# Starting the linear branch's states beside attention, and three pauses in attention's first steps

## The chip, the cores and the metric

The kernel runs on one core of a Trainium2 chip. The metric is the device time of one execution in microseconds (us). Five engines work side by side, each through its own queue in order: TensorE (PE, with its weight loads as PEld), VectorE (DVE), ScalarE (ACT), GpSimd (POOL) and SyncE (SP), which issues most of the DMAs.

## What is computed

One inference step of a two-layer backbone on 128 context tokens and 256 latent tokens, 384 columns in all, in float32. Each layer normalises its input, projects it once, runs three token mixers, merges them by sigmoid gates, and ends in a feed-forward part. The mixers are a windowed attention with a sink, a bidirectional gated linear attention (GLA), and a pooling mixer:

```python
o_a = _latent_attention(_rope_2d(qa), _rope_2d(ka), va, kc, vc, sink)
o_b, _, _ = _gla_bidir(qb, kb, vb, la_f, la_b, st[:, 0], st[:, 1])
o_b = _rmsnorm(o_b, p['g_gla_out']).reshape(B, T, GLA_VW) * jax.nn.silu(rb)
o_c = _pool_mix(uc, p['w_pool'], p['pool_scale'])
mixed = (jax.nn.sigmoid(ga) * (o_a @ p['w_br_a']) + jax.nn.sigmoid(gb) * (o_b @ p['w_br_b'])
         + jax.nn.sigmoid(gc) * (o_c @ p['w_br_c']))
# in the GLA, per chunk:
inter = jnp.einsum('bhtd,bhde->bhte', q_ * jnp.exp(b_), S)
S_new = jnp.exp(b_[:, :, -1, :])[..., None] * S + jnp.einsum('bhsd,bhse->bhde', k_ * jnp.exp(b_last - b_), v_)
```

The final GLA states of the context tokens are an output too.

## The kernel before

**Segments.** The order of the whole program is written out by hand, as a list of segments. A segment takes one unit of weights (128x1024 values) and does its matmuls (`mm3`, line 219: 24 matmuls of 384 columns). Each float32 weight is split into a high part `wh` (ACT, line 151) and a low part `wl` (DVE, line 155); `pump` puts out the split on ACT ahead of a segment, and `run_low` the subtraction on DVE, as a rule in the middle of the next segment.

**Threads and ticks.** Everything that isn't a weight product lives in generators. `tick` first puts out what stands in `self.late` (`flush`), then advances every thread to its next `yield`, in the order in which the threads were started. A segment ticks twice: in the middle (after 12 of 24 matmuls in `mm3`; after 16 of 24 in the products of a branch, `b_fn`, line 1429) and at its end. After the middle tick comes `run_low`. In `b_fn` the two evacuations `finish` on DVE (line 1443) come after the last matmul and so ahead of the end tick. What a thread puts into `self.late` at a middle tick is put out at the start of the end tick, and what it puts there at an end tick at the start of the next middle tick.

In this text ticks are counted from the end of the segment that starts attention (tick 1). Four segments of the GLA's values follow (ticks 2 to 9), four of `rb` (10 to 17), and branch c (18 to 41), six ticks for each of its four parts: two gates (`g0`, `g1`) and a product `b_fn`. So middle ticks are even; the middle ticks of `b_fn` in branch c are 22, 28, 34 and 40, its end ticks 23, 29, 35 and 41. Branch a has its first two gates at ticks 42 to 45; its first product begins with `before_a`, which joins attention, and has ticks 46 and 47.

**Attention** (`attn`) goes through 24 heads-by-blocks in steps s = 0 to 29, one to a tick, from tick 13 on. An even step scores two heads (two matmuls into two banks that are held until the exponentials are put out; mask, row maximum and its scaling on DVE, lines 1078 to 1082) and multiplies the probabilities of an earlier pair with the values (`pv`, line 1120). An odd step puts out the exponentials of the pair (line 1091). Every step from 4 on transposes one head's probabilities (`trans`, line 1109), which ACT copies out (line 1110), and every step from 2 on scales one head's (lines 1097 to 1099). The output of `pv` is split by `split_out`: the high part by ACT at once (line 251), the low part by DVE through `self.late` (line 252). Both read the same PSUM bank.

**The GLA** (`gla`) started 20 ticks earlier and comes ahead of attention in each tick. Its products of ticks 18, 24 and 29 (96 small matmuls, line 762) fill two banks each, which DVE reads by `copy_predicated` (line 838). At tick 30 the copies of line 859 are due, and then it waits for attention. Behind that wait lie the states: their decays (lines 867 to 880), eight transposes (line 891) into two banks, copied out by ACT (line 893), the state products (line 906) into two banks, read by ACT (line 909) and DVE (line 915), and the decays of the queries (lines 923 and following). After them it waits again, at line 933, for attention and for `c_done`, which `before_a` sets, and then makes the branch's output.

**PSUM.** All these small products share four banks (`psa`), handed out in turn, without those that are held. Whoever gets a bank waits until all readers of its former content are done. The threads get their banks in the order of emission, so a thread that takes more or fewer steps shifts who follows whom.

Of the kernel before, what the change touches and what calls it, by code (L numbers as in the profile page):

```python
# [30 lines left out]
class Kern:  # L31
# [715 lines left out]
    def gla(self, l, st):  # L747
# [109 lines left out]
                yield  # L857
        for j in range(4):
            nc.vector.tensor_copy(A[32 * j:32 * j + 32, :, 32 * j:32 * j + 32], Dg[32 * j:32 * j + 32])
        while not st.get("attn_done"):  # L860
            yield

        S0 = [self.t(f"S0{d}", [128, 2, 128]) for d in range(2)]
        for d in range(2):
# [138 lines left out]
    def attn(self, l, st):  # L1003
# [62 lines left out]
        def score(u):  # L1066
            blk, j, v = units[u]
            W = 128 if blk == 0 else 384
            kk = st["k"][:, 0:128] if blk == 0 else st["KA"]
            hs = slice(64 * v, 64 * v + 64)  # L1070
            h = v * 4 + j
            ps = self.psa(hold=True)
            bank = (self.sa_i - 1) % 4
            nc.tensor.matmul(ps[:, 0:W], q[hs, j, blk * 128:blk * 128 + 128], kk[hs, :])  # L1074
            if blk:
                mt = 2 - blk
                msl = ps[:, mt * 128:mt * 128 + 128]
                nc.vector.tensor_tensor(msl, msl, self.amask[:, blk - 1, :], op=ALU.add)
            nm = self.t("nm", [128, 4], bufs=4)
            nc.vector.tensor_reduce(nm[:, 0:1], ps[:, 0:W], axis=AX.X, op=ALU.max, negate=True)  # L1080
            r = rsq[:, blk * 16 + j * 4 + v:blk * 16 + j * 4 + v + 1]
            nc.vector.scalar_tensor_tensor(out=nm[:, 0:1], in0=nm[:, 0:1], scalar=r,
                                           in1=self.nsink[:, l, h:h + 1], op0=ALU.mult, op1=ALU.min)
            prob[u] = ps, nm, W, r, h, bank

        def expo(u):
            ps, nm, W, r, h, bank = prob[u]
            self.held.remove(bank)
            e = self.t("pr", [128, T], bufs=4)
            nc.scalar.activation(nm[:, 2:3], nm[:, 0:1], AF.Exp, bias=self.sink[:, l, h:h + 1])  # L1090
            nc.scalar.activation(e[:, 0:W], ps[:, 0:W], AF.Exp, bias=nm[:, 0:1], scale=r,
                                 accum_out=nm[:, 1:2])
            prob[u] = e, nm, W

        def scale(u):
            e, nm, W = prob[u]
            nc.vector.tensor_tensor(nm[:, 1:2], nm[:, 1:2], nm[:, 2:3], op=ALU.add)
            nc.vector.reciprocal(nm[:, 3:4], nm[:, 1:2])
            nc.vector.tensor_scalar(e[:, 0:W], e[:, 0:W], nm[:, 3:4], None, op0=ALU.mult)

        def trans(u):
            blk, j, v = units[u]
            nk = 1 if blk == 0 else 3
            e = prob.pop(u)[0]
            if v == 0:
                pTs[u // 2] = self.t("pT", [128, 2, T], bufs=2)
            ps = self.psa()
            for c in range(nk):
                nc.tensor.transpose(ps[:, c * 128:c * 128 + 128], e[:, c * 128:c * 128 + 128], self.ident)  # L1109
            nc.scalar.activation(pTs[u // 2][:, v, 0:nk * 128], ps[:, 0:nk * 128], AF.Copy)  # L1110

        def pv(w):
            blk, j, _ = units[2 * w]
            vidx = (0,) if blk == 0 else (1, 2, 3)
            qs = slice(blk * 128, blk * 128 + 128)
            pT = pTs.pop(w)
            ps = self.psa()
            for c in range(len(vidx)):
                for v in range(2):
                    nc.tensor.matmul(ps[64 * v:64 * v + 64, 0:128], vt[:, vidx[c], 64 * v:64 * v + 64],  # L1120
                                     pT[:, v, c * 128:c * 128 + 128], start=c == 0, stop=c == len(vidx) - 1,
                                     tile_position=(0, 64 * v))
            self.split_out(oah[:, j, qs], oal[:, j, qs], ps[:, 0:128])
# [3 lines left out]
        for s in range(n + 6):  # L1127
            if 4 <= s < n + 4:
                trans(s - 4)
            if s % 2 and s <= n:  # L1130
                expo(s - 1)
                expo(s)
            if s >= 6 and s % 2 == 0:
                pv((s - 6) // 2)
            if 2 <= s < n + 2:
                scale(s - 2)
            if s < n and s % 2 == 0:

                score(s)
                score(s + 1)  # L1140
            yield
        st["attn_done"] = True

    def pool_mix(self, l, st):
# [598 lines left out]
```

## Time and profile before

| | us |
|---|---|
| median of 3 runs | 1327.56 (1325.98 to 1328.98) |
| the profiled execution | 1326.22 |
| its span | 1324.4 |
| its PE busy | 1291.9 (98% of the span) |
| its DVE busy | 852.9 (64%) |
| its ACT busy | 596.1 (45%) |
| its mean granted clock | 0.996 of full speed |

PE is busy nearly everywhere; the time is what PE has to do and the places where it waits. A row of a timeline gives the start in us, the duration, the engine, the line, the operation with output and inputs, how many instructions are merged, and in brackets for how long the engine stood idle before it and who ended that.

### The profile page before, as it was taken

What the parts mean: (1) busy time and instruction counts of PE and PEld (TensorE: products, weight loads), DVE (VectorE), ACT (ScalarE), POOL (GpSimd) and SP (SyncE); (2) the same over time, 40 slices, a digit from 0 to 9 for tenths busy, and PEclk for the clock granted to TensorE, in tenths of its full rate; (3) what the DMA queues carried; (4) which work ended last, traced back from release to release, by engine and by line L of the source; (5) the groups of instructions that cost most, each with busy time, mean ns of one, the idle gap of its engine ahead of it and who ended that gap; (6) DMA issues with size and microseconds to landing.
All of it is one profiled execution on the core that took longest, in us unless ns stands there. A gap on an engine that the chain in (4) does not pass through costs nothing.

```text
span 1324.4 us, 23404 instructions
## 1 busy us (share of the span) xinstructions
PE 1291.9 (98%) x9285; PEld 1201.2 (91%) x9285; DVE 852.9 (64%) x1522; ACT 596.1 (45%) x1102; POOL 139.7 (11%) x190
## 2 busy tenths in 40 slices
PE   7999999999999999999999999999999999999998
PEld 5797788889998999999988887888999899999998
DVE  4497876454568768676877888754556787544432
ACT  5655455343366333333446646543435643333221
POOL 1142000010033000000222400001102300000000
PEclk9999999999999999999999999999999999999999
DMA  9943545556444656665645545355444266444442
GB/s 288 248 118 98 146 127 143 156 134 199 135 127 115 192 173 198 184 198 166 201 129 151 149 114 142 114 166 139 111 127 128 84 201 189 135 126 123 134 127 61
DMA packets 297788, 198.51 MB, mean 150 GB/s; under 512 B 24560, under 2 KB 282384, under 8 KB 297680
## 3 DMA queue, kind: packets, MB, share of 16 engines
q1 hardware_dynamic: 296928, 196.68, 52.7%
q8 instruction: 73, 1.20, 0.4%
q0 software_dynamic: 608, 0.28, 0.1%
q14 instruction: 35, 0.29, 0.1%
q10 hardware_dynamic: 144, 0.07, 0.0%
HBM read 194.64 MB, written 2.36 MB: 149 GB/s over the span
## 4 chain that ended last, share of the span: by engine, by line
PE 87%; DVE 6%; DMA 2%; issue 2%; SPq 1%; ACT 1%; POOL 1%; ACTq 0%; POOLq 0%; DVEq 0%
PE d L219 65%; PE d L1429 7%; PE d L1361 2%; DMA m<-in_w_mod_dram 2%; PE m L472 1%; PE s L1120 1%; PE s L1109 1%; PE s L1074 1%; DVE wl L155 1%; PE s L762 1%; DVE nm L1080 1%; PE s L949 1%; SPq L1181 1%; DVE ev L656 1%; PE s L943 1%
## 5 line engine op out<-in xcount | busy, mean ns | idle before, releaser
L155 DVE TENSOR_TENSOR wl<-raw,wh 128x1024 fp32r<-128x1024 f32 (+2 forms) x274 | 328.5, 1202 | 126.3 <-ACT wh L151 122.2
L151 ACT ACTIVATE wh<-raw 128x1024 fp32r<-128x1024 f32 (+2 forms) x276 | 280.0, 1017 | 172.6 <-PE d L219 63.6
L219 PE MATMUL d<-hl,wh 128*128 128x384 f32 x1248 | 252.9, 341 | 0.0
L219 PE MATMUL d<-hh,wh 128*128 128x384 f32 x1248 | 248.2, 342 | 2.0 <-DVE vf L624 2.0
L219 PE MATMUL d<-hh,wl 128*128 128x384 f32 x1248 | 243.0, 338 | 0.0
L219 PEld LDWEIGHTS d<-hh,wh 128*128 128x128 f32 x1248 | 216.0, 189 | 16.9 <-issue 10.9
L219 PEld LDWEIGHTS d<-hl,wh 128*128 128x128 f32 x1248 | 218.2, 189 | 2.0 <-issue 0.3
L219 PEld LDWEIGHTS d<-hh,wl 128*128 128x128 f32 x1248 | 219.8, 189 | 0.0
L219 PE MATMUL d<-m,wh 128*128 128x384 f32 x896 | 166.0, 337 | 0.0
L219 PEld LDWEIGHTS d<-m,wh 128*128 128x128 f32 x896 | 155.7, 188 | 0.4 <-issue 0.4
L251 ACT ACTIVATE m<-tt 128x384 fp32r<-128x384 f32 x60 | 31.3, 525 | 157.4 <-DVE tt L1531 125.7
L219 PE MATMUL d<-m,wl 128*128 128x384 f32 x448 | 87.5, 337 | 0.0
L219 PEld LDWEIGHTS d<-m,wl 128*128 128x128 f32 x448 | 78.6, 188 | 0.0
L1429 PE MATMUL d<-m,wh 128*128 128x384 f32 x384 | 72.2, 341 | 0.0
L1429 PEld LDWEIGHTS d<-m,wh 128*128 128x128 f32 x384 | 66.0, 188 | 6.6 <-issue 5.8
L710 DVE SCALAR_TENSOR_TENSOR x<-d,modT,x 128x128 f32<-128x128 f32 x64 | 23.6, 413 | 53.9 <-PE d L219 46.1
L1412 ACT ACTIVATE tt<-d 128x384 f32<-128x384 f32 x48 | 23.6, 491 | 72.4 <-PE d L219 62.5
L1449 POOL TENSOR_TENSOR m<-m,tt 128x384 f32<-128x384 f32 x16 | 16.9, 1081 | 368.7 <-DVE tt L1447 368.7
L561 POOL TENSOR_TENSOR ssq<-ssq,ev 128x384 f32<-128x384 f32 x18 | 29.4, 1636 | 248.9 <-ACT ev L559 248.9
L1531 DVE TENSOR_TENSOR tt<-tt,d 128x384 f32<-128x384 f32 x42 | 23.2, 554 | 48.9 <-PE d L219 48.6
L1518 ACT ACTIVATE tt<-d 128x384 f32<-128x384 f32 x42 | 20.6, 490 | 67.1 <-PE d L219 63.2
L1110 ACT ACTIVATE pT<-s 128x384 f32<-128x384 f32 (+1 forms) x48 | 20.1, 418 | 60.5 <-PE s L1109 60.5
(319 smaller groups left out, 1607.2 us busy)
## 6 DMA issues: line engine op xcount, KB each, us to landing
raw<-in_w_mod_dram SPq DMA_DIRECT2D x80, 512.0 KB, 3.8
raw<-in_w_in_dram SPq DMA_DIRECT2D x76, 512.0 KB, 4.0
raw<-in_w_ff_gate_dram SPq DMA_DIRECT2D x44, 512.0 KB, 4.8
raw<-in_w_ff_up_dram SPq DMA_DIRECT2D x44, 512.0 KB, 4.6
raw<-in_w_ff_down_dram SPq DMA_DIRECT2D x32, 448.0 KB, 4.4
m<-in_w_mod_dram SPq DMA_DIRECT2D x16, 512.0 KB, 7.1
raw<-in_w_in_dram SPq DMA_DIRECT2D x32, 256.0 KB, 3.9
raw<-in_w_out_dram SPq DMA_DIRECT2D x16, 512.0 KB, 4.0
```

The lines of the kernel that those rows point to most:

```text
L151: nc.scalar.activation(h[:, f], w[:, f], AF.Copy)
L155: e.tensor_tensor(l[:, f], w[:, f], h[:, f].bitcast(F32), op=ALU.subtract)
L219: nc.tensor.matmul(ps, w[:, k * width + col:k * width + col + 128], xs[xi](k0 + k), start=first and n == 0, stop=last and n == tot - 1)
L251: self.nc.scalar.activation(h, v, AF.Copy)
L561: e.tensor_tensor(self.ssq, self.ssq, sq, op=ALU.add)
L710: nc.vector.scalar_tensor_tensor(out=self.x[n][:, c0:c1], in0=ps[:, c0:c1], scalar=self.modT[l][:, fg + n, v:v + 1], in1=self.x[n][:, c0:c ...
L1110: nc.scalar.activation(pTs[u // 2][:, v, 0:nk * 128], ps[:, 0:nk * 128], AF.Copy)
L1361: nc.tensor.matmul(vps[c], (self.hl if z else self.hh)[kk][:, c * 128:c * 128 + 128], w[:, k * 512:k * 512 + 512], start=kk == 0 and w is ...
L1412: nc.scalar.activation(tt, ps[:, 0:T], AF.Tanh, scale=0.5)
L1429: nc.tensor.matmul(ps[i], w[:, k * 256 + i * 128:k * 256 + i * 128 + 128], x2[xi](k), start=w is h and xi == 0 and k == 0, stop=w is lo an ...
L1518: nc.scalar.activation(tt, pg, AF.Tanh, scale=0.5)
L1531: nc.vector.tensor_tensor(tt, tt, pu, op=ALU.mult)
```

## The change

The GLA no longer waits for attention at line 860: it gives up one tick and goes on with its states. Attention gives up one tick more after its steps 1, 3 and 5, so that each of the first three pairs of heads takes three ticks and not two.

```diff
         for j in range(4):
             nc.vector.tensor_copy(A[32 * j:32 * j + 32, :, 32 * j:32 * j + 32], Dg[32 * j:32 * j + 32])
-        while not st.get("attn_done"):
-            yield
+        yield
 
         S0 = [self.t(f"S0{d}", [128, 2, 128]) for d in range(2)]
@@
                 score(s)
                 score(s + 1)
             yield
+            if s % 2 and s < 6:
+                yield
         st["attn_done"] = True
```

## Rows read from the trace of the kernel before

**Rows 1.** PE's waits over the whole span: total us, times, longest
```profile
PE s L1109 <- DVE Dg L838: 6.3, 4, 2.8
...
PE s L762 <- DVE m L252: 1.0, 2, 0.5
PE s L1074 <- ACT pr L1091: 0.8, 2, 0.4
```

**Rows 2.** Timeline of PE in layer 0, ticks 18 and 19
```profile
157.39 0.55 PE L1109 MATMUL s<-ident,pr 128*128 128x128 f32 x3 [2.76 <-DVE Dg L838]
...
161.42 0.49 PE L1109 MATMUL s<-ident,pr 128*128 128x128 f32 x3
```

**Rows 3.** Timeline of DVE in layer 0, the copies of tick 18
```profile
156.97 0.63 DVE L838 COPY_PREDICATED Dg<-masks,s 128x192 f32<-128x192 uint8 x2
```

**Rows 4.** Timeline of PE in layer 1, ticks 18 and 19
```profile
807.79 0.55 PE L1109 MATMUL s<-ident,pr 128*128 128x128 f32 x3 [2.72 <-DVE Dg L838]
...
810.26 0.49 PE L1109 MATMUL s<-ident,pr 128*128 128x128 f32 x3
```

**Rows 5.** Stretches: us, busy (instructions) of PE, PEld, DVE, ACT, POOL, PEclk, DMA, GB/s
```profile
157.40:161.40 4.00, 4.00 (x15) 3.94 (x16) 2.62 (x8) 2.16 (x7) 0.00 (x0) 0.57 0.21 38
...
700.70:703.00 2.30, 0.35 (x2) 0.04 (x2) 2.30 (x6) 1.55 (x4) 0.70 (x1) 1.00 0.74 214
704.10:707.50 3.40, 3.40 (x11) 2.79 (x10) 2.41 (x9) 2.55 (x8) 0.00 (x0) 0.50 0.78 205
```

**Rows 6.** Timeline of DVE and of PE in layer 0 at tick 24
```profile
180.59 0.28 DVE L252 TENSOR_TENSOR m<-s,m 128x128 fp32r<-128x128 f32 x1
...
181.02 0.95 PE L762 MATMUL s<-m 64*32 64x32 f32 x88 [0.49 <-DVE m L252]
```

**Rows 7.** Timeline of PE, layer 0: an even step (tick 27), then a product's end
```profile
192.09 0.49 PE L1109 MATMUL s<-ident,pr 128*128 128x128 f32 x3
192.51 0.88 PE L1120 MATMUL s<-pT,vt 128*64 128x128 f32 x12
193.32 0.92 PE L1074 MATMUL s<-KA,m 64*128 64x384 f32 x4
194.16 0.64 PE L472 MATMUL m<-raw,sc 128*32 128x256 f32 x8
...
197.86 1.64 PE L1429 MATMUL d<-m,wl 128*128 128x384 f32 x8
```

**Rows 8.** Timeline of DVE, layer 0: a product's end (tick 22), an even step's pair
```profile
174.75 1.22 DVE L155 TENSOR_TENSOR wl<-raw,wh 128x1024 fp32r<-128x1024 f32 x1
175.89 1.01 DVE L1443 SCALAR_TENSOR_TENSOR m<-tt,d 128x384 f32<-128x384 f32 x2
...
194.26 0.30 DVE L1078 TENSOR_TENSOR s<-s,amask 128x128 f32<-128x128 f32 x1 [1.39 <-PE s L1074]
...
196.38 0.28 DVE L252 TENSOR_TENSOR m<-s,m 128x128 fp32r<-128x128 f32 x1
```

**Rows 9.** Timeline of PE and of DVE, layer 0: a pair of context heads
```profile
201.69 0.49 PE L1074 MATMUL s<-kn,m 64*128 64x128 f32 x4
...
202.22 0.29 DVE L1080 TENSOR_REDUCE nm<-s 128x1 f32<-128x128 f32 x1 [0.42 <-PE s L1074]
...
203.14 0.28 DVE L252 TENSOR_TENSOR m<-s,m 128x128 fp32r<-128x128 f32 x1
```

**Rows 10.** Timelines of PE, ACT, DVE, layer 0: the states behind attention
```profile
253.24 1.03 PE L891 MATMUL s<-ident,m 128*128 128x128 f32 x8
253.87 1.09 ACT L893 ACTIVATE m<-s 128x512 f32<-128x512 f32 x2 [0.97 <-PE s L891]
...
259.14 1.97 PE L906 MATMUL s<-m,m 128*64 128x128 f32 x32
260.70 0.61 DVE L915 SCALAR_TENSOR_TENSOR S<-S,tot,s 128x128 f32<-128x128 f32 x2 [6.32 <-ACT ev L909]
```

**Rows 11.** Timeline of ACT in layer 0: a weight split that waits for its transfer
```profile
155.65 1.06 ACT L151 ACTIVATE wh<-raw 128x1024 fp32r<-128x1024 f32 x1 [4.19 <-DMA raw<-in_w_br_c_dram]
```

## The prediction

> **What bounds the kernel now.** I read the page's busy shares first: PE works nearly all of the span, so a change of order that removes no matmul can only move the places where PE waits and the stretches of half clock that follow. Then PE's list of waits. In the part that the change touches it names three kinds, each once or twice to a layer [rows 1]: transposes of attention that wait for DVE's `copy_predicated` (6.3 us in 4 waits), GLA products that wait for DVE's low part of a `pv` (1.0 in 2), scores that wait for an exponential (0.8 in 2). Then the timelines of PE and DVE around the long ones. At tick 18 the GLA takes two banks while two are held by scores, so the transpose of step 5 gets a bank that the GLA has just filled, and DVE reads it only when it has worked off its queue: PE stands for 2.76 us in layer 0 [rows 2] and 2.72 in layer 1 [rows 4]. DVE comes to the two copies only at 156.97 [rows 3], and has no gap ahead of them.
>
> In layer 0 the pause also costs clock: the stretch behind it was granted 0.57 on the mean [rows 5], that is 1.2 GHz in most of it, and from the late transpose to the next one it took 4.03 us [rows 2] against 2.47 for the same work in layer 1 [rows 4], where the clock stayed. A fall costs 1.56 us. It need not come: of three pauses of about 2 us or more, those of 2.76 and of 1.95 (2.30 less 0.35 busy, at 700.70) were followed by the lower level, that of 2.72 was not [rows 2, 4, 5].
>
> **What goes.** With the pause after step 3, tick 18 has no step of attention: the GLA takes the banks of scores 0 and 1, whose exponentials were put out at tick 14, and no transpose follows it. Ahead of the copies DVE has one scaling and two scores less. The next user of one of these banks is score 5 at tick 19, half a gate later. So the wait of tick 18 goes (2.76 and 2.72), and with it that of tick 17 (0.8 in 2: the scores now come two ticks behind the exponentials) [rows 1, 2, 4]. At tick 24 the GLA's products now meet step 8, an even one, with no bank held; the transpose takes a free bank, and its wait goes: 6.3 - 2.76 - 2.72 = 0.8 in both layers [rows 1]. The first wait of tick 24, for the low part of a `pv`, I leave as it is, 0.5 a layer: the `pv` is now two ticks older, but its low part lies behind more in DVE's queue. Removed: 5.5 + 0.8 + 0.8 = 7.1 us.
>
> **What comes.** Three extra ticks turn the parity round. From tick 22 on the even steps, with scores and `pv`, fall on middle ticks, where they fell on end ticks. That matters in `b_fn`. The low part of a `pv` of a middle tick is put out at the end tick; on DVE's queue it now lies behind the two scores of that step, the weight split `wl` of `run_low`, and the two evacuations `finish`. I followed the handing out of the banks tick by tick, from the code.
>
> Tick 29: the third products of the GLA get the bank of trans 8 (free) and that of `pv` 3, filled at tick 28, the middle of a `b_fn`. Let T be PE's arrival at tick 28. PE: transpose 0.42, `pv` 0.81, scores 0.84, the last eight matmuls 1.64 [rows 7], some 0.1 for the eight small matmuls that go to the first bank: T + 3.8. DVE: scores start at T + 1.23, the first mask 0.94 later, the low part's place 2.12 after that [rows 7, 8], so T + 4.29; but now `wl` (1.14 to the next) and two `finish` (1.01) come ahead [rows 8], then the low part 0.28, and 0.15 until PE goes on [rows 6]: T + 6.87. PE stands 3.1 us. Behind it the transpose of step 13 gets the GLA's first bank (two are held), as at tick 24 before: 0.4 [rows 1].
>
> Tick 35 is new for another reason: the states' transposes now run inside attention. They get first the bank of `pv` 6, filled at tick 34, again the middle of a `b_fn`. PE: 0.42 + 0.81 + 0.49 + 1.64 = 3.36 [rows 7, 9]. DVE: 1.23 + 0.53 to the first maximum + 0.92 for the pair [rows 9] + 1.14 + 1.01 + 0.28 + 0.15 [rows 6, 8] = 5.26. PE stands 1.9 us. Then transpose 15 takes the bank that ACT must copy out: the first copy ends 0.63 + 0.55 after the states' transposes began, which take 1.03 [rows 10]: 0.3 with the 0.15 of a release.
>
> Tick 37: the state products get banks that are free by then, but transpose 17 gets the first of them, whose readers are done at 260.70 + 0.61 = 261.31, against PE's end at 261.11 [rows 10]: 0.35 with the release.
>
> Added a layer: 3.1 + 0.4 + 1.9 + 0.3 + 0.35 = 6.05, in both 12.1 us. No row shows these waits in place. From below they are bounded by 0.5, what the same wait cost where `wl` and `finish` were not between [rows 6]; from above by one wait of ACT for a transfer (4.19 [rows 11]) on top. I take the sum, since every term of it is a row of this queue.
>
> **What costs nothing.** The states' DVE work beside attention (eight decays at tick 31, four products at 33) lies in ticks of g1 and g0, where no bank is waited for at the next tick. The three ticks put attention's last `pv` at tick 44 and its end at the very tick before `before_a`, so the join has nothing to run; without that cover it would be bare steps, of which an even one takes PE 0.42 + 0.81 + 0.84 = 2.07 us [rows 7]. The output still waits at line 933 for `c_done`; it begins at tick 46 and no longer at 53, far ahead of branch b. The states left no wait of PE behind them where they stood (ticks 44 to 52), so taking them away from there gains nothing. The loads of the incoming states and the stores of the outgoing ones move with them on SP's queue, 13 ticks earlier; a store waits there for ACT's copy, and the weights behind it on that queue are two segments ahead of their use.
>
> **The sum.** 12.1 - 7.1 = +5.0 us of waits. Clock: before, one fall in this part; after, four pauses of 1.9 to 3.1 us, of which two in three fall by the three seen, so about three: two more, 3.1 us. Together +8.1. The profiled execution took 1326.22 (span 1324.4 and 1.8 around it): 1334.3. It lies 1.3 under the median of the runs, by which it would be 1335.7. I say 1334.5.
>
> The Trainium skill speaks here too. In "TensorE: Matmul & The Clock Gate", section "HAM oscillation", it holds that pauses of TensorE are followed by work at half clock, so that their cost is larger than the pause; the trace agrees in two of three cases, as shown. If each of the four fell, the sum would be 1.56 higher; if none, 4.7 lower.
>
> **The rivals.** Gain: the new waits of ticks 29 and 35 don't come, because DVE reaches the low part before PE needs the bank. Then what is left of the added is 2 x 1.05 = 2.1, against 7.1 removed and one fall: -6.6, 1319.7. It decides at T + 3.65: the low part would have to be done by then, which is before the second maximum of the pair; it needs another order on DVE than the code gives. For it speaks that attention's first pairs get more room while DVE is fully busy. That interleaving of stages with different busiest engines gains is also what the skill says, in "Perfetto Trace Analysis", section "Optimization Strategy"; by that rule the time would fall, as in this rival. Against it: the removed waits hang on banks, and the change hands the banks out so that two others meet.
>
> Half: DVE's lag is there, but PE itself is later at the end ticks or `wl` was put out earlier; with half of 3.1 and 1.9 and one fall the sum is -0.0, 1326.2: no change.
>
> More: ACT stands in the states' part behind a weight split that waits for its transfer, as at 155.65 [rows 11], and the transposes of tick 35 or 37 wait for ACT's copy: up to 3.8 more in one layer, 1338. Before, the trace shows such waits only in ticks 13 to 18.
>
> That the change doesn't do what it says: the states would begin no earlier if something behind line 860 waited too. The values are ready at tick 9, so nothing does.
>
> **How the numbers follow.** Forecast 0.60, more 0.05, half 0.15, gain 0.20. A measurement of this kernel can tell about 0.2% (2.7 us) from no change. Faster: the gain case, 0.20. Same: the half case, 0.15. Slower: 0.65. The forecast's own range is 1329 (no fall) to 1337 (four falls, half a microsecond more at ticks 29 and 35). For 8 in 10 the range takes in the half case and a part of the gain: 1323 to 1338.
>
> **What would show it.** PE's waits of the changed kernel: no wait of a transpose at tick 18 (near 151 in layer 0); a wait of L762 for DVE L252 of about 3 us and one of L891 for DVE L252 of about 2, each in both layers; the lower clock behind most of them. DVE's timeline: L1082, L155, L1443, L1443, L252 in this order ahead of them. The prediction is wrong if these waits are under 1 us, if PE waits in the join of `before_a`, or if waits appear in branch a.

## The result: 1339.29 us, 0.9% slower

The changed kernel takes 1339.29 us (median of 4 runs, 1337.28 to 1339.48), the kernel before 1327.01 (4 runs): a ratio of 1.0093, 95% interval 1.0081 to 1.0105. The forecast was 1334.5 with a range up to 1338. The sign and the new waits of ticks 29, 35 and 37 came as forecast. Two costs stood in no term of the sum: the time lies 4.8 us above the forecast and 1.3 us above the range.

The profiled execution took 1337.28, its span is 1335.2, 10.8 longer than before. The page's first line of PE says how this is made up:

```profile
PE 1295.7 (97%) x9285; PEld 1200.6 (90%) x9285; DVE 854.4 (64%) x1522; ACT 596.9 (45%) x1102; POOL 142.3 (11%) x190
```

Span less busy time was 1324.4 - 1291.9 = 32.5 us before and is 39.5 now: 7.0 us more in which PE stands. The other 3.8 are busy time, with the same 9285 matmuls.

First the time in which PE stands. Its list of waits, the lines that the change made or altered (total us, times, longest):

```profile
PE s L762 <- DVE m L252: 7.0, 4, 2.9
...
PE s L890 <- DVE nm L1096: 3.9, 2, 2.0
...
PE s L1108 <- ACT pT L1109: 2.1, 2, 1.4
...
PE s L1108 <- DVE Dg L838: 0.8, 2, 0.4
PE s L1108 <- DVE S L914: 0.7, 2, 0.3
...
PE s L1108 <- ACT m L892: 0.5, 2, 0.3
```

They sum to 15.0 us, where the three lines of [rows 1] had 8.1. Line numbers behind 860 are one lower than before, behind the pauses one higher. The 6.3 us of [rows 1] have shrunk to 0.8, the scores' wait for the exponential is gone, and the rest is new. Where each of them stands shows PE's timeline in layer 0 (ticks 24, 29, 29, 35, 35, 37, 39):

```profile
171.08 1.01 PE L762 MATMUL s<-m 64*32 64x32 f32 x96 [0.64 <-DVE m L252]
...
194.45 0.95 PE L762 MATMUL s<-m,m 64*32 64x32 f32 x88 [2.86 <-DVE m L252]
195.79 0.47 PE L1108 MATMUL s<-ident,pr 128*128 128x128 f32 x1 [0.40 <-DVE Dg L838]
...
220.38 1.06 PE L890 MATMUL s<-ident,m 128*128 128x128 f32 x8 [1.97 <-DVE nm L1096]
221.69 0.55 PE L1108 MATMUL s<-ident,pr 128*128 128x128 f32 x3 [0.25 <-ACT m L892]
...
230.18 0.30 PE L1108 MATMUL s<-ident,pr 128*128 128x128 f32 x1 [0.34 <-DVE S L914]
...
237.88 0.33 PE L1108 MATMUL s<-ident,pr 128*128 128x128 f32 x1 [1.37 <-ACT pT L1109]
```

In layer 1 the same seven are 0.64, 2.86, 0.40, 1.98, 0.25, 0.34 and 0.69 us. Ahead of the two long ones DVE's timeline has the order that the prediction gave, the weight's low part, two evacuations, and only then the low part of the `pv` that frees the bank:

```profile
191.95 1.22 DVE L155 TENSOR_TENSOR wl<-raw,wh 128x1024 fp32r<-128x1024 f32 x1
193.09 1.01 DVE L1444 SCALAR_TENSOR_TENSOR m<-tt,d 128x384 f32<-128x384 f32 x2
194.01 0.28 DVE L252 TENSOR_TENSOR m<-s,m 128x128 fp32r<-128x128 f32 x1
...
219.95 0.28 DVE L252 TENSOR_TENSOR m<-s,m 128x128 fp32r<-128x128 f32 x1
```

(The list names `nm` for the wait of tick 35, an instruction that ends a few hundredths after this low part at 219.95 and has no part in the bank.)

The wait of tick 39 is one that I had not summed. Timelines of SP and of ACT ahead of it:

```profile
229.42 1.26 SPq L909 DMA_DIRECT2D out_new_state_gla_dram<-ev  x2
230.78 0.41 SPq L1182 DMA_DIRECT2D raw<-in_w_in_dram  x1
```

```profile
229.88 0.39 ACT L908 ACTIVATE ev<-s 128x256 f32<-128x256 f32 x1 [0.49 <-PE s L905]
...
235.66 1.06 ACT L151 ACTIVATE wh<-raw 128x1024 fp32r<-128x1024 f32 x1 [3.59 <-DMA raw<-in_w_in_dram]
236.62 1.04 ACT L927 ACTIVATE m<-m 128x1024 f32<-128x1024 f32 x1
237.57 0.26 ACT L1109 ACTIVATE pT<-s 128x128 f32<-128x128 f32 x1
```

SP holds the stores of the states until ACT has copied them out, and issues the next weight load only behind them, at 230.78. That weight comes late: ACT stands 3.59 us at its split, then has the queries' decays, and copies the transpose for which PE waits only at 237.57.

The clock, in stretches of us with PEclk behind the five busy times:

```profile
195.70:199.10 3.40, 3.31 (x12) 3.31 (x13) 3.00 (x12) 2.37 (x8) 0.00 (x0) 0.50 0.22 64
221.70:225.10 3.40, 3.40 (x28) 3.06 (x28) 0.61 (x3) 3.25 (x10) 0.00 (x0) 1.00 0.00 0
704.10:707.50 3.40, 2.05 (x10) 1.73 (x10) 3.37 (x7) 2.90 (x7) 1.13 (x2) 1.00 0.60 152
851.00:854.40 3.40, 3.23 (x11) 3.24 (x12) 3.07 (x12) 2.30 (x8) 0.00 (x0) 0.51 0.26 77
```

1.2 GHz was granted behind both pauses of tick 29, not behind those of tick 35. The fall near 704 of [rows 5] did not come, so that this execution has two falls in the layers, as before. The other three runs were 2 us longer (1339.24 to 1339.48), at a mean granted clock of 0.992 to 0.994 against 0.996. A fall such as that at 704.10 (3.40 us at 0.50) lowers the mean by 0.5 x 3.4 / 1337 = 0.0013, so by this estimate they had one to three more. No trace shows them, and the kernel before has the same means in its own runs (0.992 to 0.997).

So the extra busy time of the profiled execution is not the clock's. Most of it is, by its rows, a neighbourhood. PE's timeline before, then after, three transposes of one head and what follows:

```profile
189.68 0.49 PE L1109 MATMUL s<-ident,pr 128*128 128x128 f32 x3
189.92 0.95 PE L219 MATMUL d<-hl,wh 128*128 128x384 f32 x4
```

```profile
176.34 0.49 PE L1108 MATMUL s<-ident,pr 128*128 128x128 f32 x3
176.76 0.64 PE L472 MATMUL m<-raw,sc 128*32 128x256 f32 x8
```

Ahead of a weight product three transposes cost 0.24 us, ahead of the modulation's small matmuls (line 472, which `filler` puts out at the end of gates) 0.42; a single transpose 0.03 and 0.20 to 0.25. (Ahead of the 128*64 matmuls of a `pv` they cost 0.42 too [rows 7].) Attention's odd steps, whose last matmul is a transpose, now lie on end ticks, where the filler follows. Before, this neighbourhood did not occur; now it does seven times a layer (four with three transposes, three with one): 4 x 0.18 + 3 x 0.2 = 1.3, in both layers 2.6 of the 3.8. The page "TensorEngine Tiling (Array Packing)" of the Trainium skill, section "Key Properties", holds that a change of the tiling mode drains TensorE; a change from 128*128 to another tiling is what these rows have in common, and about 0.2 us is what it shows here.

### The profile page after: what moved, and what is told of

Same layout as the page of the kernel before. It is cut to its first block, busy times and chain, and to the rows that moved or that the text cites. A ratio compares the mean times of both kernels' runs of the same rounds, so it can differ in the third digit from the quotient of the medians.

```text
span 1335.2 us, 23413 instructions
## 1 busy us (share of the span) xinstructions
PE 1295.7 (97%) x9285; PEld 1200.6 (90%) x9285; DVE 854.4 (64%) x1522; ACT 596.9 (45%) x1102; POOL 142.3 (11%) x190
## 4 chain that ended last, share of the span: by engine, by line
PE 88%; DVE 4%; DMA 2%; ACT 2%; issue 2%; SPq 1%; POOL 1%; ACTq 0%; DVEq 0%; POOLq 0%
PE d L219 64%; PE d L1430 7%; PE d L1362 3%; DMA m<-in_w_mod_dram 2%; PE m L472 2%; PE s L1073 1%; PE s L1119 1%; PE s L1108 1%; PE s L762 1%; DVE wl L155 1%; PE s L948 1%; DMA raw<-in_w_in_dram 1%; DVE ev L656 1%; PE s L942 1%; SPq L1182 1%
## 5 line engine op out<-in xcount | busy, mean ns | idle before, releaser
L498 DVE SCALAR_TENSOR_TENSOR A<-raw,sc,A 128x1024 f32<-128x1024 f32 x35 | 47.0, 1343 | 0.0
```

The lines of the kernel that those rows point to most:

```text
L498: nc.vector.scalar_tensor_tensor(out=acc, in0=self.raw[u], scalar=s, in1=acc, op0=ALU.mult, op1=ALU.add)
```

## The experiments

Two theories stood against each other. **Parity** (mine): the number of pauses decides whether attention's even steps fall on middle or on end ticks; on middle ticks they meet the GLA and each other in banks that DVE frees late. **States**: the load is the states' work beside attention. Each run has its own median of the kernel before, which lay between 1326.67 and 1327.36.

### Each half alone

The states freed, no pauses (the diff's first part alone):

```diff
-            if s % 2 and s < 6:
-                yield
```

> The first edit alone: the states run beside attention, attention has no pauses. If the loss comes from even steps on middle ticks (theory A), the bank meetings of ticks 18 and 24 stay as before (2.7 and 0.9 us a layer), ticks 35 and 37 meet banks that are free, and only a late weight behind the states' stores is new (about 1 us a layer): 1327 to 1330. If the states beside attention are the load that costs (theory B), most of the 12.3 us shows here: 1334 to 1339.

Measured: 1331.37 us (6 runs), ratio 1.0038 (1.0024 to 1.0053). PE's timeline, layer 0:

```profile
157.18 0.55 PE L1108 MATMUL s<-ident,pr 128*128 128x128 f32 x3 [2.60 <-DVE Dg L838]
...
236.14 0.43 PE L1119 MATMUL s<-pT,vt 128*64 128x128 f32 x2 [1.46 <-ACT pT L1109]
```

The old waits are all there, and the one of tick 39 besides (1.46 and 1.17 us), behind an ACT that waits 4.43 for a weight. There is no wait at ticks 29 and 35. The states alone cost some 4 us, of which 2.6 are the two waits of tick 39, and their work beside attention is not what makes PE stand at ticks 29 and 35.

The pauses alone, the states behind attention as before:

```diff
-        yield
+        while not st.get("attn_done"):
+            yield
```

> The second edit alone: three pauses, the states wait for attention as before. Theory A: the waits of tick 24 (0.64) and 29 (2.86 + 0.40) stay, those of ticks 35, 37 and 39 (about 3.3 a layer) go with the states, the old waits of ticks 17, 18 and 24 are gone, and what isn't explained by waits (about 1.4 us a layer, denser interruptions of the weight products) stays: 1327 + 2 x (3.9 + 1.4 - 4.0), about 1329.6. Theory B: no loss without the states, and the gain of the removed waits: about 1320.

Measured: 1333.20 us (4 runs), ratio 1.0042 (1.0025 to 1.0059).

```profile
194.66 1.15 PE L762 MATMUL s<-m,m 64*32 64x32 f32 x88 [2.86 <-DVE m L252]
...
221.47 0.86 PE L1109 MATMUL s<-ident,pr 128*128 128x128 f32 x3 [1.97 <-DVE nm L1097]
```

I had expected 1329.6, without the wait of tick 35. It came all the same, with 1.97 us: the bank of `pv` 6 is next in turn, and if the states don't take it, a transpose of attention does. So this wait too belongs to the pauses.

### What the waits are made of

`run_low` ahead of the middle tick in `b_fn`, so that DVE has done the weight's low part before the scores of that tick come:

```diff
                         if xi:
+                            self.run_low()
                             self.tick()
-                            self.run_low()
```

> The changed kernel, with the weight's low part put out ahead of the middle tick in every branch product, and not behind it. By the sum (scores, weight split, evacuations, low part, one behind the other on DVE) the weight split's 1.14 us leave the waits: 2.86 becomes about 1.7 at tick 29, 1.97 about 0.8 at tick 35, 0.64 nothing at tick 24, 5.9 us in both layers and perhaps a fall of the clock: 1331 to 1333. If DVE isn't the bound there: 1339.

Measured: 1331.15 us (5 runs), ratio 1.0035 (1.0022 to 1.0048), 7.7 less than the changed kernel by the ratios.

```profile
193.36 0.95 PE L762 MATMUL s<-m,m 64*32 64x32 f32 x88 [1.73 <-DVE m L252]
...
216.74 1.06 PE L890 MATMUL s<-ident,m 128*128 128x128 f32 x8 [0.94 <-DVE nm L1096]
```

2.86 became 1.73 and 1.97 became 0.94: 1.13 and 1.03 less, what `wl` takes in the queue [rows 8]. The wait is the sum of what lies ahead on DVE.

The low part of `pv` put out at once instead of at the next tick:

```diff
-            self.split_out(oah[:, j, qs], oal[:, j, qs], ps[:, 0:128])
+            nc.scalar.activation(oah[:, j, qs], ps[:, 0:128], AF.Copy)
+            nc.vector.tensor_tensor(oal[:, j, qs], ps[:, 0:128], oah[:, j, qs].bitcast(F32), op=ALU.subtract)
```

> The changed kernel, with the low part of every pv put out on DVE at once, right behind ACT's high part, and not through the late list. Theory A (the low part lies behind two scores, the weight split and two evacuations): the waits of 0.64 at tick 24, 2.86 at 29 and 1.97 at 35 go in both layers, 10.9 us, and with them one or two falls of the clock: about 1326 to 1328. If the bank is late for another reason (PE, ACT's high part), the time stays near 1339.

Measured: 1331.22 us (10 runs), ratio 1.0026 (1.0017 to 1.0035); I had expected 1326 to 1328. Timelines of PE, then of DVE:

```profile
195.00 0.55 PE L1108 MATMUL s<-ident,pr 128*128 128x128 f32 x3 [2.50 <-DVE Dg L838]
```

```profile
192.52 1.22 DVE L155 TENSOR_TENSOR wl<-raw,wh 128x1024 fp32r<-128x1024 f32 x1
193.65 1.01 DVE L1445 SCALAR_TENSOR_TENSOR m<-tt,d 128x384 f32<-128x384 f32 x2
194.58 0.64 DVE L838 COPY_PREDICATED Dg<-masks,s 128x192 f32<-128x192 uint8 x2
```

The GLA's products no longer wait, but the transpose behind them waits for the GLA's own copies, which stand behind the same `wl` and `finish`. Of 3.26 us 2.50 stay, under another name, and of tick 24's 0.64 a score's wait of 0.51 for the same copies; only tick 35's 1.97 goes for good. What is late is DVE at this point, not one instruction.

### The number of pauses

Two in place of three, with the states freed, then with the states waiting; one and four with the states waiting. The condition of the pause is the only edit beside that:

```diff
-            if s % 2 and s < 6:
+            if s % 2 and s < 4:
```

> The changed kernel with two pauses in place of three (after steps 1 and 3), so that the even steps are back on end ticks from step 4 on. Theory A: tick 18 stays free of waits, tick 24 has 0.9 a layer as the kernel before, 29 and 35 have none, no denser interruptions: 1327 less 6.3 and perhaps a fall, about 1319 to 1322, below both kernels. Theory B: the states still lie beside attention, so the time stays above 1330.

> Two pauses, and the states wait for attention as before. Theory A (bank meetings decide, the states bring only the late weight and the release at tick 37): the waits of 1.17 to 1.57 and 0.17 us that the kernel with two pauses and free states (1321.8) still has at ticks 39 and 37 go: about 1319. Theory B (the early start of the states is worth something by itself): slower than 1321.8.

> One pause only (after step 1), and the states wait for attention as in the kernel before. Parity theory: one pause turns the parity as three do, so from step 2 on the even steps lie on middle ticks. PE then waits 2.9 + 0.4 us at tick 29 and 2.0 + 0.25 at tick 35 in each layer, and the long wait of tick 18 is gone; about 1332 us, as with three pauses and waiting states (1333.2), though the end of attention lies two ticks earlier. Rival, pauses as room: each pause takes load off the first heads, and one gives about half of what two gave (before 1326.7, two 1317.6), about 1322 us, with no wait near 2.9 us.

> Four pauses (after steps 1, 3, 5 and 7), and the states wait for attention. Parity theory: an even count leaves the even steps from step 8 on at end ticks, so no wait of ticks 18, 29 and 35, as with two pauses; tick 24 has no step of attention, and its 0.9 us may go too. Attention's last product now stands directly ahead of branch a's first one, which waits for ACT's copy of it: 0.5 to 1.5 us a layer. About 1318 us (1316 to 1321). Rival, every pause beyond two costs: 1333 us or more, as with three.

With two pauses and the states freed: 1321.82 us (4 runs), ratio 0.9960 (0.9945 to 0.9975). With the states waiting:

| pauses | us (runs) | ratio to before (95%) | PE's waits over 0.2 us here, us a layer |
|---|---|---|---|
| none (the kernel before) | 1327.01 (4) | 1 | 4.0 |
| 1 | 1347.94 (4) | 1.0148 (1.0128 to 1.0168) | 7.1 |
| 2 | 1317.57 (4) | 0.9936 (0.9919 to 0.9952) | 0.9 |
| 3 | 1333.20 (4) | 1.0042 (1.0025 to 1.0059) | 5.9 |
| 4 | 1316.31 (4) | 0.9916 (0.9899 to 0.9934) | 0.65 |

The time goes up and down with the parity and not with the room. One pause has the waits of three, and one at tick 17 besides:

```profile
154.87 0.93 PE L1074 MATMUL s<-KA,m 64*128 64x384 f32 x2 [1.15 <-DVE Dg L838]
...
200.91 1.15 PE L762 MATMUL s<-m,m 64*32 64x32 f32 x88 [2.87 <-DVE m L252]
...
226.90 0.30 PE L1109 MATMUL s<-ident,pr 128*128 128x128 f32 x1 [1.98 <-DVE nm L1097]
```

I had expected these waits, less the one of tick 17, and about 1332 us. What is beyond that is mostly clock (stretches of the same kernel, columns as above):

```profile
155.40:158.80 3.40, 3.40 (x12) 3.07 (x11) 3.26 (x8) 0.00 (x0) 0.00 (x0) 0.53 0.02 5
199.50:206.30 6.80, 4.99 (x101) 4.89 (x102) 4.60 (x16) 2.91 (x8) 0.00 (x0) 0.54 0.31 80
227.30:230.60 3.30, 3.30 (x12) 3.25 (x11) 0.65 (x4) 2.40 (x8) 0.00 (x0) 0.50 0.47 140
285.30:292.10 6.80, 6.80 (x28) 5.33 (x27) 0.85 (x2) 2.19 (x9) 0.00 (x0) 0.50 0.56 155
```

With four more later on that is 34 us at a mean of 0.54, from which I estimate 34 x 0.46 = 15.6 us lost, 12.5 more than by the two falls of before. The waits are 6.2 more, the filler's neighbourhood (eight times a layer here, six of them with three transposes) 3.0; together 21.7, where it is 21.2 us slower.

With two pauses PE's wait of tick 18 is gone and nothing came for it; what is left is tick 24:

```profile
173.35 0.95 PE L762 MATMUL s<-m 64*32 64x32 f32 x88 [0.50 <-DVE m L252]
174.70 0.55 PE L1109 MATMUL s<-ident,pr 128*128 128x128 f32 x3 [0.40 <-DVE Dg L838]
```

In none of the kernels with no, two or four pauses is a transpose followed by line 472. What the parity costs in busy time show two kernels with the states freed, two pauses and then three (the one with the low part put out at once). The stretch is the same in both: layer 0, from the last matmul of line 726 to the first of line 949, with the same 1875 matmuls and no lower clock (columns as above):

```profile
60.76:251.73 190.97, 187.80 (x1875) 161.00 (x1873) 146.32 (x338) 105.95 (x229) 25.41 (x26) 1.00 0.49 137
```

```profile
60.57:255.23 194.66, 189.43 (x1875) 160.87 (x1873) 145.28 (x338) 105.89 (x229) 25.39 (x26) 1.00 0.49 136
```

PE is busy 1.63 us longer with three pauses, and 1.71 longer in the run with `wl` ahead (189.51); its waits are not in these numbers. With four, the wait of 0.5 to 1.5 us that I expected ahead of branch a didn't come.

### The stores of the states

The two stores moved behind the wait of line 933, once with three pauses and once with two, states freed in both:

```diff
+        fins = []
...
             fin = self.ev()[:, 0:256]
             nc.scalar.activation(fin, ps[:, 0:256], AF.Copy)
-            nc.sync.dma_start(self.o["new_state_gla"][0, l, d].rearrange("(i p) d e -> (p d) i e", p=2),
-                              fin.rearrange("p (i e) -> p i e", i=2))
+            fins.append(fin)
...
         while not (st.get("attn_done") and st.get("rb_done") and st.get("c_done")):
             yield
+        for d in range(2):
+            nc.sync.dma_start(self.o["new_state_gla"][0, l, d].rearrange("(i p) d e -> (p d) i e", p=2),
+                              fins[d].rearrange("p (i e) -> p i e", i=2))
```

> The changed kernel, with the two stores of the outgoing states put on SP's queue behind the wait for the gate of branch a and no longer right behind the state products. If the wait of tick 39 (1.37 and 0.69) comes from a weight that SP issues late, behind a store that waits for ACT's copy: that wait goes or falls under 0.3, ACT's wait for a weight near 235 (3.6 us) too, 1337 to 1338. If it comes from the exponential of 1.04 us ahead of the copy on ACT alone, it stays.

> Two pauses, free states, and the late stores. Theory A: the waits of 1.17 and 1.57 at tick 39 go, that of 0.17 at tick 37 and those of 0.9 at tick 24 stay: 1321.8 less 2.7, about 1319, the same as two pauses without the free states, so that the states' place is worth nothing either way. If the late weight isn't the cause: 1321.8.

Measured with three: 1335.79 us (4 runs), ratio 1.0071 (1.0056 to 1.0087), against 1.0093. SP issues the load that it had issued at 230.78 now at 219.21, ACT's timeline has the split that stood 3.59 us without a wait, and PE's wait of tick 39 is gone in both layers:

```profile
219.21 0.37 SPq L1185 DMA_DIRECT2D raw<-in_w_in_dram  x1
...
232.04 1.05 ACT L151 ACTIVATE wh<-raw 128x1024 fp32r<-128x1024 f32 x1
```

With two: 1318.37 us (4 runs), ratio 0.9939 (0.9925 to 0.9954), against 0.9960 with the stores where they were. So the stores on SP are worth 0.0021 to 0.0022, or 2.8 us. In each pair the two intervals just overlap; that both pairs give the same, and that the wait is gone from the rows, is what carries it. And with the stores out of the way, freeing the states is worth nothing: 0.9939 against 0.9936 with the states waiting.

### What is best

Two and four pauses, the states waiting, and the low part of `pv` put out at once (the same edit as above):

> Two pauses, states wait, and the low part of each pv is put out on DVE at once and not at the next tick. With two pauses alone only 0.50 + 0.40 us a layer are left in this part, at tick 24, the first of them for a low part. If that low part is late because it is put out late, 0.5 a layer goes: about 1316.5 us. Rival: DVE's own queue sets its time, or the copy_predicated behind it becomes late: 1317.5, no change, the wait under another name.

> Four pauses, states wait for attention, and the low part of each pv is put out at once. With four pauses PE waits only at tick 24 in this part, 0.65 us a layer for a low part; with two pauses the same edit took that wait away and left 0.40 for a transpose. With four pauses no transpose follows at tick 24, so nothing should be left: 1.3 us less than four pauses alone (1316.3), 1315.0. Rival: DVE's copies come later by the early low parts and a wait of 0.4 to 0.6 takes its place at tick 24 or 25: 1316, no change.

Measured: with two pauses 1315.52 us (4 runs), ratio 0.9913 (0.9897 to 0.9929); with four 1315.19 (5 runs), ratio 0.9912 (0.9898 to 0.9925). With two, the 0.50 of tick 24 is gone and the 0.40 is left, as expected; with four, PE has no wait left in this part of either layer. Against the same pauses alone the medians are 2.1 and 1.1 us lower, where waits of 1.0 and 1.3 us went; the intervals don't separate either from no change. Both beat the kernel before by 11 us.

## Why the prediction was right or wrong

**What goes: right.** The waits of ticks 17 and 18 and those of tick 24's transposes are gone, 7.1 us. That two pauses take those of ticks 17 and 18 away as well, and leave the kernel 9 us faster, shows that this part of the change is a real gain.

**What comes, by its terms:** tick 29 3.1 + 0.4, measured 2.86 + 0.40; tick 35 1.9 + 0.3, measured 1.97 + 0.25; tick 37 0.35, measured 0.34; tick 24 left at 0.5, measured 0.64. The waits of these steps were to add up to +5.0 and come to 2 x 6.46 - 8.06 = +4.9. Following DVE's queue instruction by instruction gave the size, and the run with `wl` ahead took just its 1.1 us out of both waits.

**A reason that was wrong:** tick 35 was put down to the states' transposes. The pauses alone show the same wait with an attention transpose in their place. It didn't change the sum, but it would have misled a repair.

**The first step that failed: "What costs nothing".** I looked at the stores on SP's queue, said rightly that they wait there for ACT, and let it go because the weights behind them were "two segments ahead of their use". The load behind them was issued 11.6 us late (230.78, against 219.21 with the stores moved), and its split waited until 235.66. That is the rival "More", at tick 39 and not at 35 or 37, and in both layers: 1.37 + 0.69 us of PE's time, 2.8 us by the runs with late stores. I gave it 0.05, since the trace of before showed ACT's waits for a transfer "only in ticks 13 to 18". That was misread. The states' part of before has them too: 2.99 us at 251.84 in layer 0, 3.40 at 901.09 in layer 1, and one right behind the stores themselves (timelines of SP and of ACT before):

```profile
260.69 1.26 SPq L910 DMA_DIRECT2D out_new_state_gla_dram<-ev  x2
262.00 0.46 SPq L1181 DMA_DIRECT2D raw<-in_w_in_dram  x1
```

```profile
266.04 1.06 ACT L151 ACTIVATE wh<-raw 128x1024 fp32r<-128x1024 f32 x1 [1.11 <-DMA raw<-in_w_in_dram]
```

No matmul waited for ACT there, so this cost PE nothing; beside attention, whose transposes ACT copies out, it does.

**The second step that failed: what a change of order can cost.** The prediction began from the premise that a change that removes no matmul "can only move the places where PE waits and the stretches of half clock that follow", so its sum has no term for busy time. That grew by 3.8 us, with as many matmuls and as many falls of the clock. The prediction saw that the parity turns, and followed it only to the banks, not to PE's own order. Rows of all kernels agree that transposes then stand ahead of the filler (seven a layer with three pauses, eight with one, none with none, two or four). By the stretches at full clock the parity costs 1.6 to 1.7 us of busy time in layer 0; if layer 1 is the same, that is 3.3 of the 3.8. That the filler's neighbourhood makes 2.6 of it is read from rows and not measured by itself. Without either of the two failed steps the time would have been inside the range.

**The clock: mis-sized, and lucky.** The sum had two more falls (3.1 us). The profiled execution has none more: the lower level followed two of the four long pauses and not three, and the fall at 704 stayed out. That the other runs, 2 us longer, had more is an estimate from their mean clocks, and the kernel before has such means in its own runs. Without these 3.1 us the forecast would have been 7.9 us too low and not 4.8, so the nearness of the number is in part luck. The terms as the trace has them, +4.9 and +2.1 of waits and +3.8 of busy time, bring the profiled execution to 1326.22 + 10.8 = 1337.0 (measured 1337.28).

**The rivals.** Gain (0.20) and half (0.15) fell: the two long waits came at 92 and 104% of their size. The Trainium skill's advice that interleaving may gain ("Perfetto Trace Analysis", section "Optimization Strategy") stood beside the gain case; here the part of the change that interleaves more, the states beside attention, cost 4 us alone, and was worth nothing once the stores were moved.

## What to carry to other kernels

Where threads take turns at fixed ticks and share buffers in rotation, a pause is not only room: an odd number of them moves every later step to the other kind of tick, so try the neighbouring counts before judging the idea. When work is moved earlier, list what each of its instructions holds up in its queue: the stores here, waiting on SP's queue for their producer, held the load behind them back by 11.6 us. And follow a new order on the busiest engine itself, since its own neighbours can cost time without any wait.

## What the runs showed of the hardware that was not expected

The clock's answer to a pause is not a function of its length alone. A pause of 1.97 us was followed by 2.4 GHz in the changed kernel (the stretch at 221.70), and one of 1.98 by 1.2 GHz with one pause (227.30); there even the pause of 1.15 us was followed by the lower level, and so was a stretch at 285.30 with no longer wait ahead than 0.30 us, at PE's small matmuls of branch b. All four runs of that kernel take 1344.69 to 1348.09 us, at mean clocks of 0.985 to 0.989. The plainest pair is in one execution: with the low part put out at once, the pause of tick 29 is 2.50 us in layer 0 and 2.49 in layer 1, and the stretches behind them are

```profile
195.00:198.40 3.40, 3.40 (x28) 3.20 (x30) 2.16 (x8) 2.81 (x8) 0.00 (x0) 1.00 0.56 151
845.90:849.30 3.40, 3.40 (x13) 3.40 (x14) 2.03 (x8) 2.71 (x8) 0.00 (x0) 0.51 0.52 144
```

What tells these cases apart stays open.
